# The last phase's sums and differences of tiles on VectorE alone, with GpSimd taking none of them

## The chip, the cores and the metric

The kernel runs on one core of one Trainium2 chip. The metric is the device time of one execution in microseconds, the median of three timed runs. The profile is that of one further execution of the same program, seen by the hardware profiler.

## The reference, cut to what matters

The whole computation is two blocks on a sequence of 1024 tokens with 1024 channels, all in fp32. The change lies in the end of the second block:

```
h = rms_norm_2(x, pre2_w) * (1.0 + sc2) + sh2
y = swiglu_ffn(h, ffn_w_in, ffn_w_out)
x = x + (1.0 + gt2) * rms_norm_2(y, post2_w)

def swiglu_ffn(h, w_in, w_out):
    gate, up = jnp.split(h @ w_in, 2, axis=-1)
    return (jax.nn.silu(gate) * up) @ w_out
```

Here w_in is 1024 x 5632 (gate and up of 2816 each) and w_out is 2816 x 1024. Ahead of it stands the output projection of the mixer, with its own norm and residual.

## The kernel before

Everything is kept with channels on the 128 partitions and tokens along the free dimension. Each fp32 product is made of three TensorE matmuls (`mm3`): an operand is split into a high part (an ScalarE copy into fp32r) and a low part (the difference of source and high part, on VectorE), by `split`, lines 2466 to 2469. A matmul takes a 128x128 weight block and 512 tokens.

The program has four phases, A, C, B and F, one after the other. The last is `phase_f` (line 1882): 16 products of the mixer's output weights, two norms in `mid` (one per half of the tokens), then the feed-forward part. Both matrix products of the feed-forward part are done as a 2x2 Strassen-Winograd scheme: seven products instead of eight, paid for with sums and differences of tiles. These sums and differences are what the change touches.

The first feed-forward product runs over 11 groups `g` of two blocks of gate and up. For each group `variant` (line 1807) makes seven weight variants: A0 and A1 (plain), and S1, S2, S4, S3, A22. S1 is a sum of two column halves of `up` (`sl<-ru`, line 1824), S2 and S4 are differences of `sl` and a gate tile, S3 of a gate and an up tile; all of them were made on GpSimd through `padd` and `psub` (lines 1839 to 1843), two 128x512 halves each. For g < 1 the low parts of S1, S2, S4 and S3 are GpSimd's too (`psplit`, line 1845). The moving operands B11, B21, T1, T2, B22, T3, T4 are made in `mid`: those of the second half of the tokens step by step while TensorE works on the first four groups' A0 and A1 (`first2`). T1 and T2 are VectorE differences; T3 and T4 are GpSimd differences of `res` tiles (lines 2001 and 2007). `rest(g)` then issues S1 x T1, S2 x T2, S4 x B22, S3 x T3 and A22 x T4, and writes the activated result to DRAM tiles `ffa` (lines 2095 and 2103).

The second feed-forward product is the loop from line 2259 over eight values of `n`. Weights come by `variant2` (VectorE sums `sc`, `raw` of tiles loaded from `in_wfo`); the moving operands are loaded from `ffa` into `c` tiles by `fetch` and combined by `parts` (line 2124): T1 and T2 into `tch`, T3 in place into `c`, B21 into `tch`, each one 128x512 GpSimd difference for each of the 11 `k`; T4 is split on GpSimd in two rounds of 11 pieces of 128x256. `finish` (line 2192) is the last norm and residual; in the two 256-token pieces that end the kernel, every second residual sum (line 2214) was on GpSimd.

TensorE's instructions keep the order in which they are written out. On the other engines the framework orders instructions by their place in the program and by its own estimate of readiness; each engine then runs its queue in order, and a waiting instruction holds all behind it. A ring of four high/low pairs holds weight variants; 8 PSUM banks (`mm`, `sm`) hold products. Almost all loads go through SP's queue, writes of `ffa` and `x3d` through GpSimd's. GpSimd also takes the power -0.5 of the norms (line 2538), before and after the change.

Of the kernel before, what the change touches and what calls it, by code (L numbers as in the profile page):

```python
# [8 lines left out]
F32 = mybir.dt.float32  # L9
F32R = mybir.dt.float32r  # L10
U32 = mybir.dt.uint32
AF = mybir.ActivationFunctionType
ALU = mybir.AluOpType
# [4 lines left out]
T = 1024  # L18
H = 512
# [1729 lines left out]
class PhaseF:  # L1749
# [57 lines left out]
    def variant(self, n, g, v):  # L1807

        if n == 0:
            self.fetch_raws(-1)  # L1810
        hi = self.ring.tile([P, 1024], F32R, tag="hi", name=self.name("hi"))
        lo = self.ring.tile([P, 1024], F32R, tag="lo", name=self.name("lo"))
        if v[0] == "A" and len(v) == 2:
            self.split(hi, lo, self.raws["g", 2 * g + int(v[1])])
        else:
            if v == "S1":
                self.sl[g] = self.base.tile([P, T], F32, tag="rmask", name=self.name("sl"))
            for i in range(2):
                c = slice(i * H, i * H + H)
                j = 2 * g + i  # L1820
                up, s = self.raws["u", j], self.sl[g][:, c]
                gate = self.raws.get(("g", j))
                if v == "S1":
                    self.padd(s, up[:, :H], up[:, H:])
                elif v == "S2":
                    self.psub(s, s, gate[:, :H])
                elif v == "S4":
                    self.psub(s, gate[:, H:], s)
                elif v == "S3":
                    s = self.fl.tile([P, H], F32, tag="s3", name=self.name("s3"), bufs=1)  # L1830
                    self.psub(s, gate[:, :H], up[:, :H])
                else:
                    s = up[:, H:]
                (self.psplit if g < 1 and v != "A22" else self.split)(hi[:, c], lo[:, c], s)
        self.fetch_raws(n)
        return hi, lo


    def padd(self, out, a, b):
        self.nc.gpsimd.tensor_tensor(out=out, in0=a, in1=b, op=ALU.add)  # L1840

    def psub(self, out, a, b):
        self.nc.gpsimd.tensor_tensor(out=out, in0=a, in1=b, op=ALU.subtract)  # L1843

    def psplit(self, hi, lo, src):

        self.act(hi, src, AF.Copy)
        self.psub(lo, src, hi.bitcast(F32))

    def quad(self, i, j, e, tag=None):  # L1850

# [30 lines left out]
    def phase_f(self, x):  # L1882
        nc, tc = self.nc, self.tc
# [15 lines left out]
        y = self.resid()  # L1899
# [23 lines left out]
        def mid(half):  # L1923

            if not nx:
                for g in range(2, self.LEAD):
                    spill[g] = [self.region.tile([P, H], F32, tag=f"{q}{7 - 2 * (g % 2) - i}1", name=self.name("sp")) for i in range(2) for q in "hl"]
                nx.extend(self.moving())
            hs = slice(half * H, half * H + H)
            hr = slice(half * 4, half * 4 + 4)  # L1930
            rb = [br.tile([P, H], F32, tag=f"rb{j}", name=self.name("rb")) for j in range(2)]
            xs = []
            for m in range(8):
                xs.append(br.tile([P, H], F32, tag="X", name=self.name("X"), bufs=8))
                nc.sync.dma_start(xs[m], self.x2d[m][:, hs])
            yield from wait(self.W[0])
            yield from self.rstd_rows(acc[half], rt[:, hr], rtmp[:, hr], rb[0], self.W[1])
            for m in range(8):
                yy, xc = y[m][:, hs], xs[m]
                self.stt(yy, yy, c1[:, m : m + 1], rb[0], ALU.mult, ALU.mult)  # L1940
                self.add(yy, yy, xc)
                nc.gpsimd.dma_start(self.x3d[m][:, hs], yy)
                accum(acc2[half], m, yy)
                yield from wait(self.W[2])
            yield from wait(self.W[3])
            yield from self.rstd_rows(acc2[half], rt[:, hr], rtmp[:, hr], rb[1], self.W[4])


            def scaled(k):
                t = y[k][:, hs]  # L1950
                self.stt(t, t, c2[:, k : k + 1], rb[1], ALU.mult, ALU.mult)
                return t, self.mods[:, 24 + k : 25 + k]

            def put(name, hi, lo):
                xv.setdefault(name, []).append((hi, lo))
                return hi, lo

            def shifted(name, t, s, hi, lo):
                put(name, hi, lo)
                self.act(hi, t, AF.Identity, bias=s)  # L1960
                self.stt(lo, t, s, hi.bitcast(F32), ALU.add, ALU.subtract)

            def tile2(tags):
                return [br.tile([P, H], F32R, tag=t, name=self.name("tv"), bufs=8 if t == "X" else 1) for t in tags]

            def tile1(j):
                t = self.hpool.tile([P, T], F32R, tag=f"h{j}", name=self.name("tv"))
                return t[:, :H], t[:, H:]

            if half == 0:  # L1970
                for k in range(8):
                    t, s = scaled(k)
                    shifted("B11" if k < 4 else "B21", t, s, nx[0][k][0], nx[1][k][0])
                    if k >= 4:
                        self.act(t, t, AF.Identity, bias=s)
                    yield from wait(2)
                return
            h0 = slice(0, H)
            for k in range(4):
                t1, s = scaled(k)  # L1980
                t = y[k][:, h0]
                self.sub(t, t1, t)
                self.split(*put("T1", nx[0][k][1], nx[1][k][1]), t)
                self.act(t1, t1, AF.Identity, bias=s)
                yield from wait(2)
            for k in range(4):
                t2, s = scaled(k + 4)
                self.act(t2, t2, AF.Identity, bias=s)
                t = y[k][:, h0]
                self.sub(t, t2, t)  # L1990
                self.split(*put("T2", *tile2(("X", "X"))), t)
                yield from wait(2)

            while "lead" not in st:
                yield
            for k in range(4):
                self.split(*put("B22", nx[0][k + 4][1], nx[1][k + 4][1]), y[k + 4][:, hs])
                yield from wait(2)
            for k in range(4):
                t = y[k][:, hs]  # L2000
                self.psub(t, y[k + 4][:, hs], t)
                tags = (("acc0", "acc1"), ("acc0b", "acc1b"), ("rb0", "rb1"))
                self.split(*put("T3", *(tile2(tags[k]) if k < 3 else tile1(0))), t)
                yield from wait(2)
            for k in range(4):
                t = y[k + 4][:, h0]
                self.psub(t, y[k][:, h0], t)
                self.split(*put("T4", *tile1(1 + k)), t)
                yield from wait(2)

# [96 lines left out]
        made, fetched, tch = {}, {}, {}  # L2107
# [16 lines left out]
        def parts(upto, dst=None):  # L2124
            while cnt[1] < min(upto, len(items)):
                n, k = items[cnt[1]]
                cnt[1] += 1
                v, t0, t1 = self.XV[n]
                f = fetched.pop((n, k))
                t = f[0] if f else tch[k][:, t0:t1]  # L2130
                if v == "T1":
                    t = tch[k] = self.sp.tile([P, H], F32, name=f"tch{k}")
                    self.psub(t, f[0], f[1])
                elif v == "T2":
                    t = tch[k]
                    self.psub(t, f[0], t)
                elif v == "T3":
                    self.psub(t, f[0], f[1])
                elif v == "B21":
                    self.psub(tch[k], tch[k], t)  # L2140
                d = dst
                if d is None:
                    d = [self.sp.tile([P, H], F32R, tag=q, name=self.name(q), bufs=AHEAD + 1)[:, : t1 - t0] for q in ("ah", "al")]
                made[n, k] = d
                (self.psplit if v == "T4" else self.split)(*d, t)

        def early_parts():
            fetch(3)
# [43 lines left out]
        def finish(t0, t1):  # L2192
# [4 lines left out]
            xs = []  # L2197
# [13 lines left out]
            for m in range(8):  # L2211
                t = yv[m, half][:, o : o + n]
                self.stt(t, t, c3[:, m : m + 1], rb, ALU.mult, ALU.mult)
                (nc.gpsimd if t1 < T and m % 2 else nc.vector).tensor_tensor(out=t, in0=t, in1=xs[m], op=ALU.add)
                nc.sync.dma_start(self.out[m][:, t0:t1], t)
                if t1 == T and m % 2:
                    yield
# [360 lines left out]
```

## Time and profile before

| | |
|---|---|
| median of three runs | 2270.28 us (2265.58 to 2273.81) |
| profiled execution, its own time | 2265.43 us |
| its span in the trace | 2263.6 us |
| mean granted TensorE clock | 0.986 |
| TensorE busy | 2192.0 us (97%) |
| VectorE busy | 1514.4 us (67%) |
| ScalarE busy | 903.3 us (40%) |
| GpSimd busy | 394.7 us (17%) |

Times in views of the trace are counted from the start of the span. In the views PE is TensorE's matmuls, PEld its weight loads, DVE is VectorE, ACT ScalarE, POOL GpSimd, SPq the queue of the engine that issues the loads. L2423, L2435 and L2455 are the lines of helpers for a VectorE sum, a VectorE operation with a scalar, and a matmul, so that groups are told apart by the names of their tiles. "Idle before" is the engine's idle time just ahead of an instruction and what ended it.

### The profile page before, as it was taken

How to read it: one execution, taken by the hardware profiler on the slowest of the kernel's cores; microseconds unless marked ns; L12 is line 12 of the kernel's file. 1: busy time of each engine (PE TensorE's matmuls, PEld its weight loads, DVE VectorE, ACT ScalarE, POOL GpSimd, SP SyncE). 2: the span in 40 equal slices, each digit the busy share in tenths (PEclk: the TensorE clock that was granted, in tenths of full speed). 3: DMA queues.
4: the chain of work that ended last, by engine and by line, in shares of the span. 5: the costliest groups of instructions: out<-in, count | busy, mean ns of one | idle time of the engine just before them, and what ended most of it. 6: DMA issues, size and time to landing. Idle time of an engine off the chain costs nothing.

```text
span 2263.6 us, 29466 instructions
## 1 busy us (share of the span) xinstructions
PE 2192.0 (97%) x10998; PEld 1807.4 (80%) x10998; DVE 1514.4 (67%) x2160; ACT 903.3 (40%) x1522; POOL 394.7 (17%) x388
## 2 busy tenths in 40 slices
PE   8999999999999999999999999999799999999896
PEld 7888788887888988878887778887578888887676
DVE  6675686777486535558555346858977676779697
ACT  5553453344255544234253222446423232334343
POOL 1000000001112200000000000011745343425245
PEclk9999999999999999999999999999899999999998
DMA  4111116321743343255454255654233222267754
GB/s 172 34 44 40 40 51 205 103 61 29 224 144 115 98 145 136 98 170 166 152 172 143 79 183 181 202 180 153 88 123 110 84 84 84 98 228 253 246 177 160
DMA packets 149815, 297.59 MB, mean 131 GB/s; under 512 B 21520, under 2 KB 43936, under 8 KB 149416
## 3 DMA queue, kind: packets, MB, share of 16 engines
q1 hardware_dynamic: 135128, 271.33, 37.2%
q0 software_dynamic: 8128, 20.07, 2.5%
q10 hardware_dynamic: 6416, 4.31, 0.7%
q8 instruction: 87, 1.43, 0.3%
q14 instruction: 56, 0.46, 0.1%
HBM read 232.55 MB, written 61.90 MB: 130 GB/s over the span
## 4 chain that ended last, share of the span: by engine, by line
PE 76%; DVE 10%; DMA 5%; issue 5%; ACT 2%; POOL 2%; SPq 0%; POOLq 0%; ACTq 0%; DVEq 0%
PE mm L2455 56%; PE sm L2455 19%; DVE lo L2423 2%; DVE al L2423 1%; PE sm L2464 1%; DVE sc L2423 1%; DMA c<-ffa 1%; DVE res L2435 1%; DVE acc L2423 1%; POOL res L1843 1%; ACT hi L2449 0%; DVE B L2435 0%; DVE rl L2435 0%; DMA raw<-in_wfo 0%; ACT C L2449 0%
## 5 line engine op out<-in xcount | busy, mean ns | idle before, releaser
L2455 PE MATMUL mm<-rh,hi 128*128 128x512 f32 x1552 | 625.6, 403 | 1.1 <-DVE res L2423 0.7
L2455 PE MATMUL mm<-rl,hi 128*128 128x512 f32 x1552 | 606.2, 391 | 1.8 <-DVE rl L2423 1.8
L2455 PE MATMUL mm<-rh,lo 128*128 128x512 f32 x1552 | 606.7, 391 | 0.0
L2455 PEld LDWEIGHTS mm<-rh,hi 128*128 128x128 f32 x1552 | 292.5, 188 | 72.8 <-issue 9.5
L2455 PEld LDWEIGHTS mm<-rh,lo 128*128 128x128 f32 x1552 | 292.2, 188 | 62.8
L2455 PEld LDWEIGHTS mm<-rl,hi 128*128 128x128 f32 x1552 | 292.7, 189 | 61.7 <-issue 3.1
L2449 ACT ACTIVATE hi<-raw 128x1024 fp32r<-128x1024 f32 (+2 forms) x189 | 182.7, 970 | 369.3 <-PE mm L2455 265.7
L2423 DVE TENSOR_TENSOR lo<-raw,hi 128x1024 fp32r<-128x1024 f32 (+2 forms) x189 | 218.4, 1159 | 112.6 <-ACT hi L2449 110.3
L2455 PE MATMUL mm<-yr,hi 128*128 128x512 f32 x384 | 118.8, 390 | 0.2 <-DVE yr L2435 0.2
L2455 PE MATMUL mm<-tv,hi 128*128 128x512 f32 x312 | 102.5, 408 | 14.0 <-DVE tv L2423 7.1
L2455 PE MATMUL mm<-hi,rh 128*128 128x256 f32 (+1 forms) x384 | 110.7, 288 | 0.0
L2455 PE MATMUL mm<-hi,rl 128*128 128x256 f32 (+1 forms) x384 | 109.2, 284 | 0.0
L2455 PE MATMUL mm<-lo,rh 128*128 128x256 f32 (+1 forms) x384 | 109.2, 284 | 0.0
L1840 POOL TENSOR_TENSOR sl<-ru 128x512 f32<-128x512 f32 x22 | 37.1, 1689 | 315.7 <-DMA ru<-in_wfi 315.7
L2538 POOL TENSOR_TENSOR hss<-hss,mhalf 128x4 f32<-128x4 f32 x16 | 16.8, 1047 | 398.2 <-DVE hss L2441 292.1
L2455 PEld LDWEIGHTS mm<-tv,hi 128*128 128x128 f32 x312 | 61.1, 197 | 31.1 <-DVE tv L2423 9.4
L2455 PEld LDWEIGHTS mm<-yr,hi 128*128 128x128 f32 x384 | 72.1, 188 | 16.1 <-DVE yr L2435 1.1
L2449 ACT ACTIVATE hi<-sl 128x512 fp32r<-128x512 f32 x66 | 39.3, 626 | 108.9 <-PE sm L2455 66.6
L2435 DVE SCALAR_TENSOR_TENSOR adaa<-adar,cact,adaa 128x512 f32<-128x512 f32 x84 | 62.8, 747 | 29.8 <-DMA adar<-in_adaw 28.9
L2455 PEld LDWEIGHTS mm<-hi,rh 128*128 128x128 f32 x384 | 73.4, 191 | 1.7 <-issue 1.2
L2455 PE MATMUL mm<-yr,lo 128*128 128x512 f32 x192 | 74.7, 389 | 0.0
L2455 PEld LDWEIGHTS mm<-hi,rl 128*128 128x128 f32 x384 | 73.5, 191 | 0.7 <-issue 0.2
(526 smaller groups left out, 4356.7 us busy)
## 6 DMA issues: line engine op xcount, KB each, us to landing
raw<-in_w SPq DMA_DIRECT2D x60, 512.0 KB
adar<-in_adaw SPq DMA_DIRECT2D x96, 256.0 KB
c<-ffa SPq DMA_DIRECT2D x88, 256.0 KB
raw<-in_wfo SPq DMA_DIRECT2D x40, 512.0 KB
raw<-in_wfi SPq DMA_DIRECT2D x30, 512.0 KB
raw<-in_wo SPq DMA_DIRECT2D x24, 512.0 KB
ru<-in_wfi SPq DMA_DIRECT2D x22, 512.0 KB
raw<-in_wpj SPq DMA_DIRECT2D x32, 256.0 KB
```

Of the source, the lines that this page charges most:

```text
L1840: self.nc.gpsimd.tensor_tensor(out=out, in0=a, in1=b, op=ALU.add)
L1843: self.nc.gpsimd.tensor_tensor(out=out, in0=a, in1=b, op=ALU.subtract)
L2423: self.nc.vector.tensor_tensor(out=out, in0=a, in1=b, op=op)
L2435: self.nc.vector.scalar_tensor_tensor(out=out, in0=a, scalar=s, in1=b, op0=op0, op1=op1)
L2449: self.nc.scalar.activation(out=out, in_=a, func=f, scale=scale, **kw)
L2455: self.nc.tensor.matmul(out, lhsT=l, rhs=r, start=start, stop=stop)
L2464: self.nc.tensor.transpose(out, a, self.ident[:n, :n])
L2538: self.nc.gpsimd.tensor_tensor(out=out, in0=tmp, in1=self.mhalf[:, : out.shape[1]], op=ALU.pow)
```

## The change

All 178 GpSimd sums (148 of 128x512, 30 of 128x256) and differences of the last phase become VectorE's, with the same operands in the same places of the program; the three GpSimd helpers go.

```diff
                 if v == "S1":
-                    self.padd(s, up[:, :H], up[:, H:])
+                    self.add(s, up[:, :H], up[:, H:])
                 elif v == "S2":
-                    self.psub(s, s, gate[:, :H])
+                    self.sub(s, s, gate[:, :H])
                 elif v == "S4":
-                    self.psub(s, gate[:, H:], s)
+                    self.sub(s, gate[:, H:], s)
                 elif v == "S3":
                     s = self.fl.tile([P, H], F32, tag="s3", name=self.name("s3"), bufs=1)
-                    self.psub(s, gate[:, :H], up[:, :H])
+                    self.sub(s, gate[:, :H], up[:, :H])
                 else:
                     s = up[:, H:]
-                (self.psplit if g < 1 and v != "A22" else self.split)(hi[:, c], lo[:, c], s)
+                self.split(hi[:, c], lo[:, c], s)
...
-    def padd(self, out, a, b):
-        self.nc.gpsimd.tensor_tensor(out=out, in0=a, in1=b, op=ALU.add)
-
-    def psub(self, out, a, b):
-        self.nc.gpsimd.tensor_tensor(out=out, in0=a, in1=b, op=ALU.subtract)
-
-    def psplit(self, hi, lo, src):
-
-        self.act(hi, src, AF.Copy)
-        self.psub(lo, src, hi.bitcast(F32))
...
-                self.psub(t, y[k + 4][:, hs], t)
+                self.sub(t, y[k + 4][:, hs], t)
...
-                self.psub(t, y[k][:, h0], t)
+                self.sub(t, y[k][:, h0], t)
...
-                    self.psub(t, f[0], f[1])
+                    self.sub(t, f[0], f[1])
                 elif v == "T2":
                     t = tch[k]
-                    self.psub(t, f[0], t)
+                    self.sub(t, f[0], t)
                 elif v == "T3":
-                    self.psub(t, f[0], f[1])
+                    self.sub(t, f[0], f[1])
                 elif v == "B21":
-                    self.psub(tch[k], tch[k], t)
+                    self.sub(tch[k], tch[k], t)
...
-                (self.psplit if v == "T4" else self.split)(*d, t)
+                self.split(*d, t)
...
-                (nc.gpsimd if t1 < T and m % 2 else nc.vector).tensor_tensor(out=t, in0=t, in1=xs[m], op=ALU.add)
+                self.add(t, t, xs[m])
```

## Rows read from the trace of the kernel before

**Rows 1.** The page, part 1: busy us, share of the span, instructions

```profile
PE 2192.0 (97%) x10998; PEld 1807.4 (80%) x10998; DVE 1514.4 (67%) x2160; ACT 903.3 (40%) x1522; POOL 394.7 (17%) x388
```

**Rows 2.** Busy time by stretch: us, PE, PEld, DVE, ACT, POOL, PEclk, DMA share, GB/s

```profile
1585.00:1645.00 60.00, 41.67 (x152) 30.23 (x151) 57.51 (x60) 28.88 (x50) 44.24 (x27) 0.86 0.26 82
1685.00:2000.00 315.00, 315.00 (x1390) 260.81 (x1391) 226.86 (x296) 95.45 (x150) 122.18 (x101) 1.00 0.29 99
2050.00:2085.00 35.00, 31.47 (x134) 24.39 (x133) 33.87 (x26) 13.13 (x19) 23.52 (x13) 1.00 0.68 230
2127.00:2142.00 15.00, 10.43 (x47) 8.30 (x45) 0.00 (x0) 2.85 (x4) 5.49 (x5) 0.94 0.67 216
2160.00:2200.00 40.00, 35.27 (x147) 27.61 (x146) 38.29 (x42) 17.17 (x28) 18.95 (x12) 0.96 0.45 147
2200.00:2240.00 40.00, 37.82 (x271) 35.63 (x270) 36.87 (x45) 21.31 (x41) 25.69 (x22) 1.00 0.56 184
2240.00:2263.60 23.60, 8.07 (x54) 6.70 (x53) 14.90 (x36) 1.88 (x5) 7.46 (x9) 0.70 0.41 134
```

**Rows 3.** Waits from 1500 us to the end: us in total, times, longest

```profile
POOL c L1843 <- DMA c<-ffa: 18.6, 7, 4.0
...
PE mm L2455 <- DVE al L2423: 12.8, 5, 9.3
...
PE mm L2464 <- DVE acc L2423: 11.3, 3, 4.8
```

**Rows 4.** VectorE in order of time, two runs of 128x512 differences

```profile
1618.07 5.11 DVE L2423 TENSOR_TENSOR res<-res,res 128x512 f32<-128x512 f32 x3
...
1633.75 2.49 DVE L2423 TENSOR_TENSOR tv<-res,tv 128x512 fp32r<-128x512 f32 x4
```

**Rows 5.** GpSimd in order of time, in the same stretch

```profile
1614.20 8.43 POOL L1843 TENSOR_TENSOR res<-res,res 128x512 f32<-128x512 f32 x5 [0.63 <-DVE res L2423]
...
1636.31 1.29 POOL L1840 TENSOR_TENSOR sl<-ru 128x512 f32<-128x512 f32 x1 [8.64 <-DMA ru<-in_wfi]
```

**Rows 6.** VectorE groups from 1585 to 1645: busy us, mean ns, idle before

```profile
L2423 DVE TENSOR_TENSOR tv<-res,tv 128x512 fp32r<-128x512 f32 x11 | 12.7, 1179 | 0.0
L2435 DVE SCALAR_TENSOR_TENSOR res<-res,c,rb 128x512 f32<-128x512 f32 x8 | 9.3, 1185 | 1.0 <-ACT rb L2449 1.0
...
L2423 DVE TENSOR_TENSOR res<-res,res 128x512 f32<-128x512 f32 x4 | 6.9, 1753 | 0.0
L2435 DVE SCALAR_TENSOR_TENSOR sp<-C,sp 128x512 f32<-128x512 f32 x4 | 6.0, 1494 | 0.0
L2423 DVE TENSOR_TENSOR sp<-sm,sp 128x512 f32<-128x512 f32 x4 | 2.7, 678 | 0.0
```

**Rows 7.** GpSimd's line 1843 by stretch: us, busy (instructions), clock, DMA, GB/s

```profile
1585.00:1645.00 60.00, 40.32 (x24) 0.86 0.26 82
...
1685.00:2000.00 315.00, 75.76 (x49) 1.00 0.29 99
...
2050.00:2085.00 35.00, 23.52 (x13) 1.00 0.68 230
...
2160.00:2200.00 40.00, 17.93 (x11) 0.96 0.45 147
2200.00:2240.00 40.00, 25.00 (x21) 1.00 0.56 184
```

**Rows 8.** VectorE in order of time, around the T3 stage of the second product

```profile
2142.64 1.23 DVE L2423 TENSOR_TENSOR raw<-raw,ru 128x1024 f32<-128x1024 f32 x1 [15.73 <-issue]
```

**Rows 9.** SP's queue in order of time, in the same stretch

```profile
2128.98 8.81 SPq L2122 DMA_DIRECT2D c<-ffa  x5
2137.84 0.43 SPq L1857 DMA_DIRECT2D raw<-in_wfo  x1
```

**Rows 10.** VectorE in order of time, the last norm and residual

```profile
2254.87 0.87 DVE L2435 SCALAR_TENSOR_TENSOR yz<-yz,c,mm 128x256 f32<-128x256 f32 x2 [1.31 <-PE mm L2455]
...
2259.01 0.42 DVE L2214 TENSOR_TENSOR yu<-yu,X 128x256 f32<-128x256 f32 x1
```

**Rows 11.** GpSimd in order of time, its last residual sum

```profile
2259.17 0.83 POOL L2214 TENSOR_TENSOR yu<-yu,X 128x256 f32<-128x256 f32 x1 [0.28 <-DVE yu L2435]
```

## The prediction, made before the change was run

> **What bounds the kernel now.** The page's busy times come first [rows 1]: TensorE is busy 97% of the span, VectorE 67%, GpSimd 17%. Read so, an edit between VectorE and GpSimd is worth nothing. But the share is a mean over the program, so the next view is the busy time by stretch of the last phase, the only one that the change touches [rows 2]. It falls into three kinds. From 1685 to 2000 us TensorE is busy for 315.00 of 315 us: nothing can be won there, only lost. From 1585 to 1645 TensorE is busy for 41.67 of 60 us, and VectorE for 57.51: VectorE's queue sets the pace while the moving operands T1 to T4 are made. In the second feed-forward product the same happens in shorter places: from 2050 to 2085 TensorE idles 3.5 us with VectorE at 33.87 of 35, from 2160 to 2200 it idles 4.7 with VectorE at 38.29 of 40, from 2200 to 2240 it idles 2.2 with VectorE at 36.87 of 40. From 2127 to 2142 it idles 4.6 us while VectorE does nothing at all, which is a wait for a load. The list of waits agrees: TensorE's longest single one is 9.3 us on an `al` tile, and three waits on `acc`, the sums of squares, make 11.3 us [rows 3].
>
> The third view is the two engines in order of time. Four VectorE differences with GpSimd silent take 2.49 us; one alone reads 0.68, as the `sp<-sm,sp` group [rows 6], so they follow each other 0.60 apart ((2.49 - 0.68) / 3). Three others, with GpSimd at work beside them, take 5.11 us, 1.70 each, and the five GpSimd differences of that time take 8.43 us, 1.69 each [rows 4, 5]. One of each in every 1.70 us: they take turns. The groups of the stretch say the same by operand [rows 6]: those with both inputs in SBUF read 1.18, 1.19, 1.75 and 1.49 us, while `sp<-sm,sp`, whose one input is a PSUM tile, keeps 0.68. So in this program a GpSimd tile operation is not free for VectorE: when both queues are full it costs VectorE 1.70 - 0.60 = 1.10 us, and doing it on VectorE itself would cost 0.60.
>
> **The change part by part.** 178 operations move, and GpSimd keeps only the norms' powers and its DMAs. No DMA moves to another queue.
>
> *The stretch of T1 to T4, 1585 to 1645.* 26 operations leave GpSimd: 24 of line 1843 [rows 7] and two of line 1840, one of them in [rows 5]. At full alternation the gain is 26 x (1.10 - 0.60) = 13.0 us. Not all of them met a VectorE operation, so I take the stretch's own balance: 60 VectorE instructions 0.60 apart are 36 us, against 57.51 measured [rows 2], so 21.5 us are turns given to GpSimd, 0.83 for each moved one. They go, and 26 x 0.60 = 15.6 come back: -5.9 us. The lower bound of the gain is 0, if the new queue order puts T3 and T4's differences ahead of T2's; the upper one is TensorE's idle time there, 18.3 us. I take 6, the balance, since VectorE is nearly without a gap.
>
> *The first product's steady part, 1685 to 2000.* 49 operations of line 1843 [rows 7], and by the code a third of that again for S1 (line 1840), so 65 x 0.60 = 39 us at most on VectorE, beside 88 us in which it is idle [rows 2]. TensorE is without a gap and the result is 0. What hides it is that slack; without it the cost would be up to 39 us less the turns saved (65 x 0.83 = 54), so nothing in any case but a wait.
>
> *The second product's T2 stretch, 2050 to 2085.* 13 operations [rows 7], at most 13 x 0.50 = 6.5 us, and by the balance's share of the first stretch (0.83 - 0.60 = 0.23 each) at least 3.0. TensorE's idle time caps it at 3.5. I take 3.
>
> *The T3 stretch, 2110 to 2160.* Here VectorE stands for 15.73 us at `raw<-raw,ru` until its load lands [rows 8]; that load is issued at 2137.84, behind five `c` loads that take SP 8.81 us [rows 9], because each needs a `c` tile that a T3 difference gives back. With the difference at 0.60 instead of the 1.29 of an unhindered GpSimd operation [rows 5], five links are 3.5 us shorter at best. On the other side the T3 differences waited seven times for `c` loads, 18.6 us in all [rows 3], on an engine that nobody else needed; on VectorE the `al` and `lo` tiles for TensorE are queued behind each such wait. Since VectorE is standing there anyway, I take 0, with +18.6 and -3.5 as the ends.
>
> *The B21 and T4 stretches, 2160 to 2240.* 11 operations before 2200, with the same two prices 2.5 to 5.5 us, under a cap of 4.7: I take 2.5. After 2200, 21 of 128x256. The last residual's 16 operations of that size (12 on VectorE) take VectorE from 2254.87 to 2259.43, 4.56 us or 0.38 each with GpSimd beside it [rows 10], so 21 x 0.38 = 8 us at most are added, against 25.00 us of GpSimd work whose turns go [rows 7]; TensorE's idle 2.2 us is the cap. I take 1.
>
> *The end.* VectorE ends at 2259.43 and GpSimd's last sum at 2260.00 [rows 10, 11]. All 16 on VectorE are 16 x 0.38 = 6.1 us, with GpSimd's turns still counted in the 0.38, so they end at 2261.0 at the latest, 1.0 later; without the turns less. I take +0.5.
>
> Sum: -6 + 0 - 3 + 0 - 2.5 - 1 + 0.5 = -12 us. The profiled execution took 2265.4 us; the median of the runs shown is 2270.3, 4.9 above it. From the profile the sum gives 2253.4, from the median 2258.3. I forecast 2255, between the two.
>
> At VectorE's load of 96% in the first stretch (57.51 of 60) [rows 2], its two-input groups read up to 1.75 instead of 0.68 us [rows 6]. The Trainium skill, "Perfetto Trace Analysis", section "Optimizing Scalar/DVE Operations", says that when VectorE is saturated, work given to ScalarE or even GpSimd may help, and adds that the port which GpSimd and VectorE share may take the help away. By the first half the stretch would become longer by the whole 15.6 us, by the second it would become shorter as summed above; the rows favour the second.
>
> **The rivals.**
>
> *The gain is off the path.* The stretch 1585 to 1645 may be held by the chain T2 needs (scale, bias on ScalarE, difference, high part, low part, four times) and the T3 stall may stay where it is because loads set it, eating what comes before. For it: the load rate from 2127 to 2142 (216 GB/s with VectorE idle), the wait of 15.73 us. Against: VectorE has hardly a gap in the first stretch. Then half of the first term and the last ones remain: -3 - 1 + 0.5, 2262 from the profile, 2267 from the median: about 2265.
>
> *VectorE stands before loads (slower).* A GpSimd operation that waits for a load holds only GpSimd. The sum `sl<-ru` waited 8.64 us at 1636 [rows 5]; in VectorE's queue it would hold drains of PSUM and T3's low parts, and the first term becomes -6 + 8.6 = +2.6. In the T3 stretch the 18.6 us are added. Sum: 2.6 - 3 + 18.6 - 2.5 - 1 + 0.5 = +15: 2280 to 2285. For it: both waits are in the rows, and the order in the queue follows an estimate, not the chip. Against: VectorE waits in T3 already, so most of the 18.6 us overlap its 15.73. It decides where over 12 us of these waits are not hidden.
>
> *More than the sum.* T2's differences stood in turns with those of T3 and T4, which TensorE needs later [rows 4, 5]; if the one queue puts T2 first, and TensorE's clock (0.86 there [rows 2]) no longer falls, most of the 18.3 us go, say 14, and the caps are reached after: -14 - 3.5 - 3.5 - 4.7 - 2.2 + 0.5 = -27: about 2240.
>
> *Offloading pays when VectorE is full.* If GpSimd's turns did not hold VectorE, what is added counts in full where VectorE bounds: 15.6 + 13 x 0.60 + 11 x 0.60 + 8 = +38: about 2305. Against it stand 1.75 beside 0.68 us in one stretch [rows 6]. The Trainium skill's sentence above is this case.
>
> **How the numbers follow.** Chances: the forecast 0.53, more than the sum 0.17, off the path 0.18, VectorE before loads 0.11, offloading pays 0.01. A measurement of this kernel tells a change from none at about 0.3%, 7 us. Faster by that: the first two cases, 0.70. Within: off the path, 0.18. Slower: 0.12. The forecast's own range is 2246 to 2263 (the terms between half and the caps, and the 4.9 us between profile and median). For 8 in 10 it reaches over nearly all of the off-the-path case, to 2271, and over half of the larger gain, to 2238: 0.53 + 0.1 + 0.17 = 0.8.
>
> **What would show it.** Right, if in the profile after VectorE's two-input operations of 512 columns read 0.68 us everywhere in the last phase, its busy time over the phase stays about level although 178 operations came to it, and TensorE's idle time from 1585 to 1645 falls from 18 to about 12 us. The turns are wrong as the cause if these groups stay over 1 us. The forecast fails high if VectorE shows long idle times ended by loads of `ru` or `c` while TensorE waits, and low if TensorE's waits in the stretch of T1 to T4 nearly vanish.

## The result and the profile after

The changed kernel takes 2229.1 us (median of 4 runs, 2227.1 to 2229.7) against 2268.2 us for the kernel before beside it: 0.9821 of its time, 95% interval 0.9802 to 0.9840. That is faster, as forecast, but by 39 us where 12 were summed, and below the stated range, which ended at 2238.

The page's part 1 of the changed kernel, which answers to [rows 1]:

```profile
PE 2178.7 (98%) x10998; PEld 1802.3 (81%) x10998; DVE 1509.3 (68%) x2338; ACT 905.6 (41%) x1522; POOL 119.9 (5%) x210
```

178 instructions came to VectorE (2160 to 2338) and its busy time fell, from 1514.4 to 1509.3 us: what the moved work takes is what the turns had taken. The VectorE groups of the changed kernel from 1581 to 1641 us, which answer to [rows 6] (busy us, mean ns):

```profile
L2412 DVE TENSOR_TENSOR res<-res,res 128x512 f32<-128x512 f32 x12 | 7.9, 680 | 0.0
L2412 DVE TENSOR_TENSOR tv<-res,tv 128x512 fp32r<-128x512 f32 x12 | 7.8, 679 | 0.0
L2424 DVE SCALAR_TENSOR_TENSOR res<-res,c,rb 128x512 f32<-128x512 f32 x8 | 5.9, 746 | 0.0
...
L2424 DVE SCALAR_TENSOR_TENSOR sp<-C,sp 128x512 f32<-128x512 f32 x4 | 2.7, 684 | 0.0
L2412 DVE TENSOR_TENSOR sp<-sm,sp 128x512 f32<-128x512 f32 x4 | 2.7, 684 | 0.0
```

The operations with two SBUF inputs read 0.68 to 0.75 us where they read 1.18 to 1.75, and the one with a PSUM input still reads 0.68. The busy times by stretch, with the columns of [rows 2]; the stretches are those of [rows 2] moved by what had been gained ahead of them. The third is shortened to the same TensorE work, and the fourth holds the work for which the kernel before took from 2127 to 2160 us:

```profile
1581.00:1641.00 60.00, 49.60 (x195) 37.66 (x194) 59.98 (x101) 31.47 (x54) 2.60 (x2) 0.94 0.24 82
1668.00:1983.00 315.00, 315.00 (x1391) 260.82 (x1391) 230.12 (x354) 95.63 (x149) 18.53 (x35) 1.00 0.28 97
2033.00:2063.00 30.00, 30.00 (x134) 24.85 (x133) 29.64 (x41) 12.20 (x18) 0.00 (x0) 1.00 0.83 281
2104.00:2126.00 22.00, 22.00 (x99) 18.22 (x98) 18.94 (x27) 8.94 (x15) 0.00 (x0) 1.00 0.75 254
2126.00:2166.00 40.00, 36.92 (x157) 29.75 (x156) 34.62 (x53) 17.06 (x27) 1.04 (x1) 0.96 0.48 157
2164.00:2204.00 40.00, 40.00 (x290) 37.99 (x289) 37.63 (x69) 21.83 (x42) 0.70 (x1) 1.00 0.56 185
```

In the first stretch TensorE idles 10.4 us instead of 18.3, and VectorE runs 101 instructions in 60 us without a gap, where it ran 60. These are the signs that the prediction named for being right; all three came, the idle time a little past its 12 us, and the time was still missed. The T2 stretch and the T3 stretch of the second product (third and fourth row) have lost all of TensorE's idle time.

**Where the time went.** TensorE's instructions have one order in all kernels of this study, so the start of the same matmul can be compared between two traces. The table takes five matmuls, which the kernel before starts at 1585, 1705, 2045, 2111 and 2167 us, its last one (2254 us) and the end of the span, and gives how much later (+) or earlier (-) than the kernel before each stretch between them was passed, in us. Each column is a difference of two such shifts, from one profile of each kernel.

```
kernel                     ahead  first  steady   T2     T3   B21,T4  end    span
changed                     -4.0  -12.7    0.0   -5.2  -12.8   -4.1   0.5   -38.5
e1_t3_back                  -3.0  -14.4    0.0   -5.2   -9.2    1.5   0.4   -29.8
e2_t3_moved                 -5.4    0.8    0.0    0.9   -9.0    4.4   0.0    -8.3
e3_mid_moved                -1.7   -4.4    0.0    2.3    1.9    1.2   0.0    -0.6
e4_variants_moved           -4.9  -10.7    0.0    0.7   -0.9    1.3   0.0   -14.5
e5_t1t2_moved               -4.2   -0.2    0.0   -5.2   -6.8    2.6   0.0   -13.8
e6_t1t2_back                 0.9  -14.3    0.0    2.1   -7.2   -1.7   0.4   -19.9
e7_idle_reads               -4.4    4.4    0.0   -5.2  -12.8   -3.0   0.4   -20.5
e8_idle_writes              -6.0  -14.3    0.0   -5.2  -12.8   -2.1   0.4   -40.1
e9_b21_t4_back               0.6  -14.3    0.0   -5.2  -12.8    1.6   0.4   -29.8
e10_last_on_gpsimd           3.5  -12.8    0.0   -5.2  -12.8   -1.3   0.0   -28.7
e11_t1t2t3_moved            -0.7   -1.0    0.0   -5.2  -12.8    2.7   0.0   -17.1
e12_more_c_tiles             0.3   -0.1    0.0    0.2    2.3    0.4   0.0     3.0
e13_weights_other_queue      2.2   -0.3    0.0    2.5  -10.0    4.7   0.0    -0.9
e14_residual_other_queue    -4.9    0.1    0.0   -0.8    1.8    0.8   0.0    -3.0
```

The first column lies nearly all in front of the change. It runs from -6.0 to 3.5 with the weight variants on VectorE and from -5.4 to 2.2 without, so it belongs to the execution, not to an edit; the change's own share between the two profiles is 34.5 us. Of the difference of the medians (39.1), 4.6 us are not placed by this.

Most other columns have noise too, since each is from one profile. Kernels that hold the same code in the first stretch lie between -12.7 and -14.4 there (changed, e1, e6, e8, e9, e10). At T2 those with nothing moved lie between -0.8 and 2.5. At B21 and T4 the four that are alike from T2 to there (changed, e7, e8, e10) lie between -4.1 and -1.3. A difference of two or three us in one of these columns shows nothing by itself.

TensorE's time between two of these matmuls is idle time and busy time. From the two traces, in us, before and changed:

```
              first           T2             T3            B21,T4
idle      18.9 -> 10.4     3.5 -> 0.0    10.0 -> 0.0    13.3 ->  9.5
busy     101.2 -> 96.9    62.5 -> 60.7   45.8 -> 43.1   73.8 -> 73.5
```

So some 26 us of the gain are idle time, and 9 are the same matmuls in less time. Of these 9, 7 lie in the first and the T3 stretch, and there the granted clock rises with it, from 0.91 to 0.97 and from 0.91 to 1.00. In the kernel before it stands at 0.50, the lower of its two levels, from 1620 to 1635, after 5 us in which TensorE was busy for 1.56, and again from 2140 to 2150, during and behind the T3 stall. In the changed kernel the lowest of eight slices of 5 us from 1601 us on is 0.66 (columns of [rows 2]; the first three lines before, the last two changed):

```profile
1620.00:1625.00 5.00, 0.89 (x2) 0.38 (x2) 5.00 (x4) 2.27 (x4) 5.00 (x4) 0.50 0.14 52
1630.00:1635.00 5.00, 5.00 (x14) 3.88 (x13) 4.87 (x9) 3.01 (x6) 0.00 (x0) 0.51 0.41 118
2145.00:2150.00 5.00, 3.28 (x8) 2.61 (x9) 4.60 (x5) 2.10 (x4) 2.08 (x2) 0.50 0.64 211
```
```profile
1611.00:1616.00 5.00, 5.00 (x14) 3.62 (x14) 5.00 (x9) 0.47 (x1) 0.00 (x0) 0.66 0.55 170
1631.00:1636.00 5.00, 5.00 (x20) 4.11 (x19) 5.00 (x9) 1.24 (x2) 0.00 (x0) 0.84 0.00 0
```

At T2 the granted clock is 1.00 in both kernels, so the 1.8 us there are not the clock's.

### The profile page after: what moved, and what is told of

The parts are those of the page before. It is cut to its first block, busy times and chain, and to the rows that moved or that the text cites. A ratio compares the mean times of both kernels' runs of the same rounds, so it can differ in the third digit from the quotient of the medians.

```text
span 2225.1 us, 29359 instructions
## 1 busy us (share of the span) xinstructions
PE 2178.7 (98%) x10998; PEld 1802.3 (81%) x10998; DVE 1509.3 (68%) x2338; ACT 905.6 (41%) x1522; POOL 119.9 (5%) x210
## 4 chain that ended last, share of the span: by engine, by line
PE 74%; issue 14%; DVE 8%; DMA 2%; ACT 2%; POOL 0%; SPq 0%; POOLq 0%; DVEq 0%; ACTq 0%
PE mm L2444 51%; PE sm L2444 21%; PE sm L2453 1%; DVE lo L2412 1%; DVE res L2412 1%; DVE res L2424 1%; DVE rl L2424 0%; DVE B L2424 0%; DVE al L2412 0%; DVE acc L2412 0%; DMA mraw<-z_mq 0%; DMA c<-ffa 0%; DMA mD<-mlrows 0%; ACT C L2438 0%; DVE rl L2412 0%
## 5 line engine op out<-in xcount | busy, mean ns | idle before, releaser
L2444 PEld LDWEIGHTS mm<-rh,lo 128*128 128x128 f32 x1552 | 291.3, 188 | 62.5
L2412 DVE TENSOR_TENSOR lo<-raw,hi 128x1024 fp32r<-128x1024 f32 (+2 forms) x189 | 209.6, 1112 | 105.1 <-ACT hi L2438 102.8
L2444 PEld LDWEIGHTS mm<-yr,hi 128*128 128x128 f32 x384 | 72.1, 188 | 16.3 <-DVE yr L2424 1.1
L2438 ACT ACTIVATE hi<-sl 128x512 fp32r<-128x512 f32 x66 | 39.1, 627 | 106.5 <-PE sm L2444 72.4
L2444 PEld LDWEIGHTS mm<-lo,rh 128*128 128x128 f32 x384 | 73.4, 191 | 0.0
L2444 PE MATMUL sm<-tv,hi 128*128 128x512 f32 x216 | 66.5, 389 | 0.0
```

The source lines that it names most:

```text
L2412: self.nc.vector.tensor_tensor(out=out, in0=a, in1=b, op=op)
L2438: self.nc.scalar.activation(out=out, in_=a, func=f, scale=scale, **kw)
L2444: self.nc.tensor.matmul(out, lhsT=l, rhs=r, start=start, stop=stop)
```

## The experiments

**T3 alone, both ways.** The first run puts it back in the changed kernel, the second moves nothing else in the kernel before.

```diff
                 elif v == "T3":
-                    self.sub(t, f[0], f[1])
+                    self.nc.gpsimd.tensor_tensor(out=t, in0=f[0], in1=f[1], op=ALU.subtract)
```
```diff
                 elif v == "T3":
-                    self.psub(t, f[0], f[1])
+                    self.sub(t, f[0], f[1])
```

> The changed kernel with the 11 T3 differences of the second product back on GpSimd, all else on VectorE. Theory (queue order): in the T3 stretch VectorE's low parts `al` stood behind a weight difference whose load waited for `c` tiles that these same low parts hold, and GpSimd's differences let that order come about; TensorE's wait of about 9 us on `al` comes back: 2236 to 2240 us. Rival (turns alone): 11 operations cost their turns, 0.5 us each at most, and no stall returns: 2229 to 2234 us. Second rival (arrival): the stall left because earlier stretches became shorter and the loads came in time; then it stays away here: 2229 to 2231 us.

> The kernel before with the 11 T3 differences alone moved to VectorE. Theory (queue order): TensorE's wait of 9.3 us on `al` is gone or under 2 us, with the stretches ahead unchanged: 2256 to 2260 us. Rival (turns alone): 2263 to 2268 us with the wait still near 9 us. Second rival (arrival): since nothing ahead is shorter, the wait stays: 2265 to 2268 us.

Measured: 2238.3 us for the first and 2261.4 for the second (0.9964 of before, 0.9951 to 0.9977), before 2267.9. TensorE in order of time at the wait on `al`, in the kernel before, in the first and in the second:

```profile
2146.72 0.80 PE L2455 MATMUL mm<-al,hi 128*128 128x512 f32 x1 [9.29 <-DVE al L2423]
```
```profile
2117.13 0.50 PE L2444 MATMUL mm<-al,hi 128*128 128x512 f32 x1 [2.97 <-DVE al L2412]
...
2150.57 0.50 PE L2444 MATMUL sm<-al,hi 128*128 128x512 f32 x1 [2.43 <-DVE al L2412]
2165.98 1.11 PE L2453 MATMUL mm<-ident,acc 128*128 128x128 f32 x4 [5.14 <-DVE acc L2412]
```
```profile
2135.39 0.50 PE L2455 MATMUL mm<-al,hi 128*128 128x512 f32 x1 [0.90 <-DVE al L2423]
2142.04 0.50 PE L2455 MATMUL mm<-al,hi 128*128 128x512 f32 x1 [0.92 <-DVE al L2423]
```

T3 alone takes the stall away with nothing shorter ahead of it, so the arrival rival and the turns rival fall there, though the time lies 1.4 us above the theory's range. But 4.4 of its 9.0 us are given back behind (table), where TensorE's wait on `acc` grows from 4.34 to 7.05 us. And the way back brings 3 us of stall, not 9: the first run's time is the theory's and its mechanism is not. There must be a second cause.

**T1 and T2 alone, both ways; then all three.**

```diff
-                    self.psub(t, f[0], f[1])
+                    self.sub(t, f[0], f[1])
                 elif v == "T2":
                     t = tch[k]
-                    self.psub(t, f[0], t)
+                    self.sub(t, f[0], t)
```

> The kernel before with the 22 T1 and T2 differences of the second product alone moved to VectorE; T3 stays on GpSimd. Theory (two causes of the T3 stall: the loads of `x3d` and `c` start late against TensorE, and each `c` tile turns round slowly through GpSimd): the stretch of T2 becomes 5 us shorter, and with the loads issued sooner against TensorE the T3 stall falls from 9.7 to 3 to 6 us: 2257 to 2261 us. Rival (turnaround alone): only the 5 us of the T2 stretch come and the stall stays near 9 us: 2262 to 2265 us.

> The changed kernel with the T1 and T2 differences back on GpSimd. Theory (two causes): the T2 stretch is 5 us longer, the T3 stall comes back only to 1 to 2 us, as where T3 alone was moved: 2234 to 2237 us. Rival (the sooner start of the loads decides): the stall is 5 us or more again: 2239 to 2244 us.

> The kernel before with T1, T2 and T3 of the second product moved to VectorE, all else on GpSimd. Theory (two causes of the T3 stall, each of which alone left 1 to 3.5 us of it): together they take all of it, so that TensorE gains 5 us in the T2 stretch and 10 to 12 in the T3 stretch, 16 us, of which up to 4 are given back at the next `acc`: 2251 to 2256 us. Rival (the two overlap, and only the variants' move as well takes the rest): the stall keeps 1 to 3 us, as after T3 alone: 2255 to 2259 us.

Measured: 2254.4, 2244.4 and 2246.5 us. T1 and T2 give 5.2 us in their own stretch in every kernel that moves them. TensorE's longest wait on `al` in the T3 stretch is 3.07 us with T1 and T2 moved alone, 2.65 with them back, and none over 0.5 us with all three. The first two of these:

```profile
2130.18 0.50 PE L2455 MATMUL mm<-al,hi 128*128 128x512 f32 x1 [3.07 <-DVE al L2423]
```
```profile
2128.99 0.60 PE L2444 MATMUL mm<-al,hi 128*128 128x512 f32 x1 [2.65 <-DVE al L2412]
```

So the first and the third run bear out two causes of the stall. In the second the wait lies between the theory's 1 to 2 us and the rival's 5 or more, and the whole T3 stretch is 5.6 us longer, so neither fits it well. The times were missed: too high by 3 us in the first and by 5 in the third, too low by 7 in the second (above the rival's range as well), where the T2 stretch became 7.3 us longer, not 5.

**What the T3 stall stands on.** Three edits of the kernel before that move no sum: four more tiles for T3's loads, the S3 weights' loads from ScalarE's queue, and the loads of the residual from it.

```diff
+                    if v == "T3" and row == k1:
+                        ts.append(self.sp.tile([P, H], F32, tag="cx", name=self.name("cx"), bufs=4))
+                    else:
+                        ts.append(fl.tile([P, H], F32, tag="c", name=self.name("c"), bufs=8)[:, : t1 - t0])
```
```diff
-            s, b = self.quad(0, 0, e), self.quad(1, 0, e, "ru")
+            s, b = self.quad(0, 0, e, None, self.nc.scalar), self.quad(1, 0, e, "ru", self.nc.scalar)
```
```diff
-                nc.sync.dma_start(xs[m], self.x3d[m][:, t0:t1])
+                (nc.scalar if t1 == T else nc.sync).dma_start(xs[m], self.x3d[m][:, t0:t1])
```

> The kernel before with four more tiles for the second operand of T3, so that its loads hold 12 tiles instead of 8; all differences stay on GpSimd. Theory (turnaround): the weight load in SP's queue stands behind `c` loads that wait for a tile; with four more it is issued sooner, and the T3 stall falls from 9.7 to under 5 us: 2259 to 2264 us. Rival (the rate of the loads or VectorE's turns set it): the stall stays at 8 us or more: 2265 to 2270 us.

> The kernel before, with the loads of the S3 weights of the second product (both operands, 12 loads) issued from ScalarE's queue instead of SP's; every sum stays where it was. Theory (order in SP's queue): the weight load that TensorE's T3 stall ends with stood behind `c` loads which waited for GpSimd's differences; from another queue it is issued as soon as its tile is free, and the stall falls from 9.7 to under 3 us: 2258 to 2264 us. Rival (rate of the loads, or low parts queued on VectorE): it stays over 6 us: 2264 to 2271 us.

> The kernel before, with the 8 loads of `x3d` for the residual of the upper 512 tokens issued from ScalarE's queue instead of SP's. Theory (these 2 MB, which wait for the tiles of the `sc` sums, hold `c` loads and weights behind them): the stall falls from 9.7 to 3 to 6 us: 2262 to 2266 us. Rival (the `c` loads hold the weights by themselves through GpSimd's differences): the stall stays over 7 us: 2265 to 2271 us.

Measured: 2264.7 us (0.9970 to 0.9996 of before), 2263.6 (0.9953 to 0.9987) and 2266.7 (0.9987 to 1.0019), before 2268.7, 2268.5 and 2268.5. The longest waits on `al` in the T3 stretch are 7.80, 1.69 and 8.02 us: more tiles and the residual's loads are not it, the weights' place in SP's queue is. In the second run 4.7 of the 10.0 us won there are given back behind, where the wait on `acc` is 7.43 us. ScalarE's queue in the second of these kernels, then SP's:

```profile
2129.06 0.37 ACTq L1857 DMA_DIRECT2D raw<-in_wfo  x1
```
```profile
2124.81 20.52 SPq L2122 DMA_DIRECT2D c<-ffa  x12
```

While twelve `c` loads take SP's queue from 2124.81 to 2145.33, the weight load is issued at 2129.06 beside them; in the kernel before it stood behind them until 2137.84 [rows 9]. What SP's queue waited for from 2095 to 2150 us, in the kernel before and with T3 alone moved:

```profile
SPq L2122 <- POOL c L1843: 12.2, 8, 1.9
SPq L2122 <- DMA c<-ffa: 9.5, 7, 2.1
```
```profile
SPq L2122 <- DVE c L2423: 3.7, 8, 0.9
SPq L2122 <- DMA c<-ffa: 2.4, 3, 1.1
```

Eight waits for T3's differences go from 12.2 to 3.7 us, and the loads themselves are waited for less. Waits for `al` grow from 9.4 to 14.6 us, so all that the `c` loads wait falls from 31.5 to 20.7 us. The same weight load in SP's queue, with T3 alone moved and in the changed kernel:

```profile
2127.95 0.38 SPq L1857 DMA_DIRECT2D raw<-in_wfo  x1
```
```profile
2103.26 0.38 SPq L1846 DMA_DIRECT2D raw<-in_wfo  x1
```

Counted from the first matmul of the T3 stretch, this load is issued at 25.8 to 28.8 us in the five kernels that have none of these differences on VectorE and issue it from SP's queue, at 19.9 to 20.4 us in the four that have either T3 or T1 and T2 there, at 14.1 to 16.3 us in the six that have all three there, and at 13.5 us from ScalarE's queue. The wait on `al` at the matmul behind it is 7.80 to 11.78 us in the first of these groups, 0.90 to 3.07 in the second, and under 0.25 in the others. The stall follows the time at which this load is issued.

**The first stretch in two parts.** In the kernel before, the eight differences of T3 and T4 in `mid` alone, and the weight variants alone (the change's hunk in `variant`).

```diff
-                self.psub(t, y[k + 4][:, hs], t)
+                self.sub(t, y[k + 4][:, hs], t)
...
-                self.psub(t, y[k][:, h0], t)
+                self.sub(t, y[k][:, h0], t)
```

> The kernel before with the 8 differences of T3 and T4 in `mid` alone moved to VectorE; the weight variants stay on GpSimd. Theory (order in the first stretch): these eight stood in turns with T2's differences, which TensorE needs first; T2 starts some 8 us sooner and 4 to 8 us of the 12.7 us that the changed kernel won in this stretch come: 2260 to 2264 us. Rival (each moved operation is worth the same): 8 of 26 operations, a third of 12.7: 2264 us, and T2 starts no more than 4 us sooner.

> The kernel before with the weight variants (S1, S2, S4, S3 and the low parts of the first group) alone moved to VectorE; T3 and T4 in `mid` stay on GpSimd. Theory (order): the eight differences of T3 and T4 still take turns with T2's, and no more than 5 to 7 us of the 12.7 come: 2261 to 2263 us. Rival (each operation the same): 18 of 26, 8.8 us: 2258 to 2260 us. Both theories expect no change from 1700 to 2000 us, and the T3 stall of the second product as before.

Measured: 2264.9 us (0.9969 to 0.9997) and 2252.8 (0.9908 to 0.9957). In the stretch 4.4 and 10.7 us, 0.55 and 0.59 for each moved operation. In the first run T2's first matmul starts only 1.0 us sooner against the start of the stretch, and its last one 9.6 us sooner. About half of that is lost again at T3, where TensorE waits 8.15 us instead of 3.37 for a PSUM bank that VectorE empties late:

```profile
1639.26 1.19 PE L2455 MATMUL mm<-tv,hi 128*128 128x512 f32 x2 [8.15 <-DVE w L2423]
```

So the order theory falls: it had 8 us for T2's start in the first run and at most 7 us for the second. The rival is nearer, and each moved operation is worth about the same, though the second run's time lies 5 us under its range too. In the first run the second product is 5.4 us longer (2.3, 1.9 and 1.2 in the table); column by column, stretches with nothing edited differ by as much, so no cause is shown for it.

**Turns by themselves.** In the changed kernel, idle work on GpSimd behind the first T1.

```diff
+                if k == 0:
+                    scr = self.fl.tile([P, H], F32, name="scr")
+                    th = nx[0][0][1].bitcast(F32)
+                    for _ in range(24):
+                        nc.gpsimd.tensor_tensor(out=scr, in0=th, in1=th, op=ALU.add)
```
```diff
+                    self.act(scr[:, :4], nx[0][0][1].bitcast(F32)[:, :4], AF.Copy)
+                    for _ in range(64):
+                        nc.gpsimd.memset(scr, 0.0)
```

> The changed kernel with 24 sums of 128x512 more on GpSimd, from the first T1 on; they read one finished tile twice and write a tile that nobody reads, so nothing waits for them and VectorE's queue keeps its instructions. Theory (turns): while they run, VectorE's operations with two SBUF inputs read about 1.7 us, one of GpSimd's to one of VectorE's, each costs VectorE 1.1 us in a stretch where it has no gap, and TensorE loses 15 to 26 us: 2244 to 2256 us. Rival (the queue's order alone made the old stretch slow): VectorE stays at 0.68 us: 2228 to 2231 us.

> The changed kernel with 64 GpSimd fills of a 128x512 tile (no input) in place of the sums of the run beside it, begun at the same first T1 by one 4-column ScalarE copy. Theory (VectorE's second input is what takes turns with GpSimd's reads, so a fill that reads nothing does not hold it): VectorE stays at 0.68 us: 2228 to 2232 us. Rival (any tile operation of GpSimd takes a turn): VectorE's operations read 1.1 us or more while the fills run, some 34 us at 0.53 each: 2240 to 2260 us.

Measured: 2249.5 and 2228.2 us. GpSimd's group, and VectorE's from 1593 to 1628 us, with the sums and then with the fills:

```profile
L1977 POOL TENSOR_TENSOR scr<-rh 128x512 f32<-128x512 f32 x24 | 33.0, 1375 | 8.4 <-ACT rh L2443 6.6
...
L2417 DVE TENSOR_TENSOR res<-res,res 128x512 f32<-128x512 f32 x4 | 6.1, 1522 | 0.0
L2417 DVE TENSOR_TENSOR tv<-res,tv 128x512 fp32r<-128x512 f32 x4 | 5.5, 1372 | 0.0
```
```profile
L1977 POOL MEMSET scr<- 128x512 f32 x64 | 33.7, 527 | 10.9 <-ACT scr L2443 7.2
...
L2417 DVE TENSOR_TENSOR res<-res,res 128x512 f32<-128x512 f32 x12 | 8.0, 696 | 0.0
L2417 DVE TENSOR_TENSOR tv<-res,tv 128x512 fp32r<-128x512 f32 x11 | 7.5, 696 | 0.0
```

33 us of sums that nobody waits for cost TensorE 17.1 us in the stretch (4.4 against -12.7), 0.71 for each; 34 us of fills cost nothing. The turns are real. A sum reads and writes and a fill only writes, so it is GpSimd's reading that takes them.

**The end of the phase.** In the changed kernel, B21's differences and T4's low parts back on GpSimd, and, by itself, four residual sums of the last 256 tokens.

```diff
-                    self.sub(tch[k], tch[k], t)
+                    self.nc.gpsimd.tensor_tensor(out=tch[k], in0=tch[k], in1=t, op=ALU.subtract)
...
-                self.split(*d, t)
+                if v == "T4":
+                    self.act(d[0], t, AF.Copy)
+                    self.nc.gpsimd.tensor_tensor(out=d[1], in0=t, in1=d[0].bitcast(F32), op=ALU.subtract)
+                else:
+                    self.split(*d, t)
```
```diff
-                self.add(t, t, xs[m])
+                (nc.gpsimd if t1 == H and m % 2 else nc.vector).tensor_tensor(out=t, in0=t, in1=xs[m], op=ALU.add)
```

> The changed kernel with the 11 B21 differences and the 22 low parts of T4 back on GpSimd. Theory (turns): the last part of the second product, which became 3.9 us shorter, goes back by that, and the stretches before it stay as in the changed kernel: 2232 to 2235 us. Rival (the full price of turns, 11 x 0.5 + 22 x 0.4): 14 us, 2241 to 2244 us. Second rival (these had been hidden): 2228 to 2231 us.

> The changed kernel with four of the eight residual sums of the last 256 tokens on GpSimd again, as before. Theory: the time from TensorE's last matmul to the end of the span, which became 0.4 us longer, becomes 0.4 shorter, and nothing else moves. Rival: the writes to DRAM set the end, and it stays within 0.1 us.

Measured: 2235.1 us for the first, at the theory's edge; its last stretch is 5.7 us longer than the changed kernel's, and 2.9 to 4.6 us longer than that of the three other kernels that are alike there. The second has one run: from the last matmul to the end it is 0.46 us shorter, as expected; its time of 2237.0 says nothing of that, since its stretch ahead of the edits was 7.5 us longer. From the last matmul to the end all kernels with these sums on VectorE read 9.86 to 9.89 us, and all others 9.43 or 9.44.

## Why the prediction was too high

**The mechanism** of the turns was right, with their price on two-input operations. They are shown by adding them (24 sums) and by removing them. The steady part gave 0, as summed. The rivals "off the path", "VectorE stands before loads" and "offloading pays" did not come; VectorE does wait for `ru` and `c` loads, 3.8 us at the longest, but no wait of TensorE on `al` is left behind. Three things were sized wrongly: the stall at T3, which put the time below the range, the first stretch, and TensorE's clock, which had no term in the sum.

**The first stretch, -6 taken, -12.7 measured.** The step that failed is "they go, and 26 x 0.60 = 15.6 come back: -5.9 us", a size. It took the new load, 36 + 15.6 = 51.6 us, from VectorE's busy 57.51, not from the stretch's 60 us, in which its short idle times went as well: -8.4. TensorE's idle time between the same matmuls did fall by 8.5. The other 4.3 us are its busy time, 101.2 to 96.9 us: the sum has no term for the granted clock, which the prediction names in a rival only. That the price of full alternation, 13.0 us, comes so near to 12.7 is luck, since it too leaves the clock out. The two partial moves gave 0.55 and 0.59 for each operation, clock included.

**The T2 stretch, -3 taken, -5.2 measured.** The cap of 3.5 us was right: TensorE's idle time in the whole stretch is 3.5 us, and all of it went. The other 1.8 us are busy time (62.5 to 60.7 us), at a granted clock of 1.00 in both; a cap taken from idle time alone leaves them out.

**The T3 stretch, 0 taken, -12.8 measured.** This is the step that put the time below the range. Of the 12.8 us, 10.0 are idle time and 2.7 are busy time, with the clock at 0.50 behind the stall in the kernel before. The wait and its load were rightly named, and "five links are 3.5 us shorter at best" was wrong: between this load and the `raw` load before it SP issues 15 `c` loads, not the five of the last row, and a `c` load also comes sooner when T1 and T2 no longer take turns. Each of the two alone gave more than half of the 12.8 (9.0 and 6.8), so they are not to be added. That the place in SP's queue makes the stall is shown by the run that only changes it. The 18.6 us of waits for `c` loads that were feared in VectorE's queue became 4.1 us with T3 alone moved and 3.3 in the changed kernel.

**B21, T4 and the end, -3.5 and +0.5 taken, -4.1 and +0.5 measured.** Right, the first within a spread of -1.3 to -4.1 in kernels that are alike there.

**"More than the sum"** was nearest in time (2240), in part by luck. Its 14 us for the first stretch came true, and the clock falls less there, as it said (to 0.66 over 5 us instead of 0.50). But its ground, T2 first in the queue, is worth little by itself, as the run that moves T3 and T4 shows, and it had 3.5 us for the T3 stretch too.

## What to carry to other kernels

Between two engines that take turns, price an operation by the turn it costs where one of them has no gap, and set the new load against the whole stretch and not against busy time. Idle time of TensorE that goes can take a low clock with it: here some 26 us of idle time went with 9 us of busy time, so the idle time is no cap on the gain. Where a stall ends with a load, follow the issuing queue back from that load as far as it has been late: whatever gives back the tiles of the loads ahead is on the path, on whichever engine it runs. A gain in one stage is partly given back at the next wait, so parts of a change are tried both alone and left out.

## What the runs show of the hardware

GpSimd's fills of 128x512 at 0.527 us, 64 in a row, left VectorE's two-input operations at 0.70 us, where sums at 1.375 us brought them to 1.52. The Trainium skill, "SBUF — State Buffer", section "Who interferes with whom", states this: a VectorE instruction with two SBUF inputs contends with a GpSimd instruction that reads SBUF and not with one that only writes. These two runs agree with it.
